# A streaming encoder layer: band writes and bias loads queued behind a weight load, a value tile released earlier, one attention step placed behind the next rows

## The chip, the cores and the metric

One NeuronCore of a Trainium2 chip runs the whole program. The metric is the device time of one execution in microseconds (us), lower is better. Of several executions the median counts.

## The reference

One layer of an encoder with three head groups reads the same normalised rows (2048 prompt rows and 8 x 16 sample rows of width 1024):

```python
qa, ka, va, ga, qb, kb, vb, gb, qm, gm = _project(x, g_pre, w_in)      # RMSNorm, then one matmul
oa = _band_attention(qa, ka, va, A_LEFT_CHUNKS, _relpos_bias(rel_bias_a, d), None)   # 6 heads, 64 + 512 keys
ob = _band_attention(qb, kb, vb, B_LEFT_CHUNKS, _alibi_bias(d), sink_b)              # 6 q heads, 2 kv heads
om = _attn_core(qm, mk, mv, None, None, None)                          # mk, mv from 256 memory rows
y  = x + rmsnorm(concat([oa * silu(ga), ob * silu(gb), om * silu(gm)]) @ w_out, g_post)
```

The sample rows do the same against caches of keys and values (512 cached keys for A, 128 for B, 256 memory keys for M). Outputs are y, and the new keys and values.

## The kernel before, in words

The prompt rows go in four groups of 512; group 0 carries the 128 sample rows too. Every float32 product is made as three products of rounded halves, so each weight tile of 128 x 1024 comes as a *pair*: `load_w` (L145 to L156) issues the DMA into `wraw` on SyncE's queue (SPq, L152), ScalarE copies the rounded upper half into `whl` (L153), and VectorE or GpSimd in turn subtracts to get the lower half (L154). There are three `wraw` and three `whl` buffers.

A group has a *dense* lane (V: value projections, Pa and Pb: key, query and gate of a head pair, K: the B keys, N: the next group's row scales, L: `load_rows` of the next group, Q: its memory queries, O: output projection) and an *attention* lane (M: memory, Sa and Sb: sample attention of a pair of A or B heads, Aa and Ab: prompt attention). The tables `DENSE` and `ATTENTION` (L43 to L50) list the steps, `AFTER` (L56 to L59) says which must be done before a step, and two generators are interleaved by their estimated cost. A scheduler in the build then fixes the order on each engine: it takes what is emitted first and is ready first in its own model of time. On the chip each engine runs its instructions strictly in that order.

Ahead of group 0 stand `first_rows`, the memory's keys and values (`memory_keys`, L328 to L343) and the sample's memory attention (`sample_m`). `memory_keys` makes two value tiles of 128 x 256 in PSUM: `split_v` (L255) makes their halves `mV` by ScalarE (L237) and VectorE (L238), and `store_T` (L296) copies them for the output (`stgT`, L298). Projections share two PSUM buffers of one tag (`psN`, `psT`), so a third tile starts only when the first is read out.

The A bias depends on the distance alone. `bands()` (L369 to L371) writes six bands `skew_d` of 128 x 768 in DRAM from a row `e_d`, and skewed reads of it give the bias tiles: `nbs` in `sample_a` (L719 to L727, 17 small loads) and `nbA` in `attn_a` (L756 to L760, four loads of 64 x 576), with three `nb` buffers. `load_rows` (L462) of group 1 loads eight column blocks (`xk`, two buffers), scales and splits them into `xn`, in place of the old rows. `next_scales` loads the next group's rows (`xt`), squares them on ScalarE and ends with small TensorE products `rb` (L183).

Names in the order rows below: `sa`, `sb` are scores, `ss` the sample's scores, `pt` and `spt` transposes, `oa`, `ob`, `so` values, `kta` and `vta` the sample's cached keys and values.

Of the kernel before, what the change touches and what calls it, by code (L numbers as in the profile page):

```python
# [53 lines left out]
PIECE = 6  # L54

AFTER = {"X1": "Aa0", "X2": "Aa1", "K0": "Aa0", "V1": "Aa0", "Pa2": "Aa1", "C0": "K0 V1 Ab0 Ab1 Ab2",  # L56
         "E0": "M0 M1 Aa0 Aa1 Ab0 Ab1 Ab2", "Aa0": "F0 V0 X0 Pa0", "Aa1": "V0 X1 Pa1", "Aa2": "V1 X2 Pa2", "Sa0": "V0 Pa0", "Sa1": "V0 Pa1", "Sa2": "V1 Pa2"}
for _j in range(3):
    AFTER[f"Ab{_j}"] = AFTER[f"Sb{_j}"] = f"K0 V1 Pb{_j}"  # L59
W_AT = {name: i for i, name in enumerate(W_TILES)}  # L60
# [3 lines left out]
def encoder_step(ctx, tc, x_p, x_s, xT0, xT, mem, memT, wt, wm, g_pre, g_mem, g_post, rel_rev, sink,  # L64
# [3 lines left out]
    pe, act, dve, pool, sp = nc.tensor, nc.scalar, nc.vector, nc.gpsimd, nc.sync  # L68
# [73 lines left out]
    vctx_d = [drp.tile([128, 4, 256], F32, name=f"vctx{i}") for i in range(6)]  # L142


    def load_w(src, hl=None):  # L145

        raw = wrawp.tile([128, 1024], F32, tag="wraw", name="wraw")
        if hl is None:
            hl = whlp.tile([128, 2, 1024], F32R, tag="whl", name="whl")
        eng = (dve, pool)[turn["s"] % 2 if turn["s"] > 4 else 0]  # L150
        for m in [slice(0, 1024)] if turn["s"] else [slice(0, 512), slice(512, 1024)]:
            sp.dma_start(out=raw[:, m], in_=src[:, m])  # L152
            act.activation(hl[:, 0, m], raw[:, m], AF.Copy)  # L153
            eng.tensor_tensor(hl[:, 1, m], raw[:, m], hl[:, 0, m].bitcast(F32), ALU.subtract)  # L154
        turn["s"] += 1
        return hl  # L156
# [139 lines left out]
    def store_T(dst, ps, n, scale=1.0):  # L296
        t = sbp.tile([128, 640], F32, tag="sb", name="stgT")
        act.activation(t[:, :n], ps, AF.Copy, scale=scale)  # L298
        sp.dma_start(out=dst, in_=t[:, :n])

    def memory_load():
        t = [xp.tile([128, D], F32, tag="x", name="mT") for _ in range(2)]
# [25 lines left out]
    def memory_keys(st):  # L328

        rk = sbp.tile([128, 640], F32, tag="sb", name="rk")[:, :256]  # L330
        act.activation(rk, row_factors(st, 2)[:, :256], AF.Copy)
        for p in range(2):
            w = load_w(wm[p])
            ps = run(project_T(w, memhl, 0, 256))
            t = sbp.tile([128, 640], F32, tag="sb", name="mkn")[:, :256]
            dve.tensor_tensor(t, ps[:, :256], rk, ALU.mult)
            split_k(mK[:, p], slice(0, 256), t)
            sp.dma_start(out=mkT[p], in_=t)
        ws = [load_w(wm[2]), load_w(wm[3])]
        for i in range(2):  # L340
            ps = run(project_N(ws, lambda a, k: memhl[:, a, k, i * 128:(i + 1) * 128]))
            split_v([mV[:, 0], mV[:, 1]], i, ps, st[:, i:i + 1])
            store_T(mv[i * 128:(i + 1) * 128], ps[:, :256], 256, st[:, i:i + 1])  # L343

    def toeplitz(h, n, c0, c1):

# [199 lines left out]
    def xg(g):  # L546
        return xnT[min(g, 1)]
# [67 lines left out]
    memory_keys(mst)  # L615
    for p in range(2):
        sample_m(p, *qg[p][1:])
    bands()

    bctx = None  # L620
    for g in range(NG):
# [14 lines left out]
        def block_v(slots, half):  # L636
            ws = [weights("v", half, r) for r in range(2)]
            for i in range(5 if g == 0 else 4):
                ps = yield from project_N(ws, lambda a, k: xg(g)[:, a, k, i * 128:(i + 1) * 128])
                if i == 4:  # L640
                    vsm = gr[:, 1280:1536] if half else mo[:, 4, 4:6].rearrange("p a b -> p (a b)")
                    act.activation(vsm, ps[:, :256], AF.Copy, scale=rs_rows[:, 4:5])
                    if half == 0:
                        sp.dma_start(out=avs[:, 0:256], in_=vsm)
                    else:
                        sp.dma_start(out=avs[:, 256:384], in_=vsm[:, 0:128])
                        sp.dma_start(out=bvs, in_=vsm[:, 128:256])
                    return [vsm[:, 0:128], vsm[:, 128:256]]
                split_v(slots, i, ps, rs_rows[:, i:i + 1] if g == 0 else None)
                if g == NG - 1:  # L650
                    t = xp.tile([128, 640], F32, tag="xk", name="stgN", bufs=2)
                    act.activation(t[:, :256], ps[:, :256], AF.Copy)
                    r0 = i * 128
                    if half == 0:
                        sp.dma_start(out=av[r0:r0 + 128, 0:256], in_=t[:, 0:256])
                    else:
                        sp.dma_start(out=av[r0:r0 + 128, 256:384], in_=t[:, 0:128])
                        if i == 3:
                            sp.dma_start(out=bv, in_=t[:, 128:256])
            return []  # L660
# [57 lines left out]

        def sample_a(pr, Q, G, ksm, vsm):  # L719
            bias = nbp.tile([128, 640], F32, tag="nb", name="nbs")  # L720
            sp.dma_start(out=bias[:, 512:576], in_=mask_new)
            for h in range(2):
                for b in range(4):
                    r = 32 * b + 16 * h
                    sp.dma_start(out=bias[r:r + 16, 0:512], in_=toeplitz(2 * pr + h, 16, 0, 512))
                    sp.dma_start(out=bias[r:r + 16, 512 + 16 * b:528 + 16 * b],
                                 in_=toeplitz(2 * pr + h, 16, 512, 528))  # L727
            kt, vt = {}, {}

            def kts(hf, b):  # L730
                if b % 2 == 0:
                    if pr == 0 or (pr == 1 and b == 2):
                        kt[0] = spare_load(b // 2, ckaT[pr, 2 * hf + b // 2])
                        kt[0] = kt[0].rearrange("p (b c) k -> p b c k", b=2)
                    else:
                        t = wrawp.tile([128, 1024], F32, tag="wraw", name="kta")
                        sp.dma_start(out=t, in_=ckaT[pr, 2 * hf + b // 2])
                        kt[0] = t.rearrange("p (b k) -> p b k", b=2)
                return kt[0][:, b % 2]

            def vts(hf, b, t):
                if b % 2 == 0 and t == 0:
                    v = xp.tile([128, D], F32, tag="x", name="vta")
                    sp.dma_start(out=v, in_=cva[pr, 2 * hf + b // 2])
                    vt[b // 2] = v.rearrange("p (b t d) -> p b t d", b=2, t=4)
                return vt[b // 2][:, b % 2, t]

            return sample_attn(pr, Q, G, kts, vts, 512, (ksm, vsm), bias, None)

        def attn_a(pr, q, G, slot, vcur, vctx=None):  # L750
            nb, held = [], {}

            def weigh(i0, h):
                if not nb:
                    for hh in range(2):
                        t = nbp.tile([128, 640], F32, tag="nb", name="nbA")  # L756
                        for p, c in ((0, 0), (64, 64)):
                            pool.memset(t[p:p + 64, 576 * (p == 0):][:, :64], BIG)
                            sp.dma_start(out=t[p:p + 64, c:c + 576], in_=toeplitz(2 * pr + hh, 128, c, c + 576)[p:p + 64])
                        nb.append(t)  # L760
                st = stp.tile([128, 16], F32, tag="st", name="sta")
                for i in (i0, i0 + 1):
# [454 lines left out]
```

## Time and profile before

| | |
|---|---|
| median of 3 runs | 1175.23 us (1174.24 to 1175.70) |
| the profiled execution's own time | 1173.39 us |
| its span | 1171.4 us |
| TensorE matmul (PE) busy | 1121.5 us, 96% |
| VectorE (DVE), ScalarE (ACT), GpSimd (POOL) busy | 803.8, 729.3, 313.2 us |
| mean granted TensorE clock | 0.991 of full speed |

The profile is one execution; 2.0 us of its own time lie outside the span. An engine's "idle before" is the wait ahead of an instruction, with the instruction that ended it. PEclk is the granted share of TensorE's full clock. SPq rows are DMA issues on SyncE's queue, and a DMA row of the chain of waits lasts from issue to landing.

### The profile page before, as it was taken

Reading aid. Unit: us, or ns where it says so; the run is one execution under the profiler, and the core shown is the slowest. Engines: PE = TensorE matmul, PEld = TensorE weight load, DVE = VectorE, ACT = ScalarE, POOL = GpSimd, SP = SyncE. Lnnn points to the kernel's source line nnn. Section 1 sums busy time; section 2 is a strip of 40 time slices with the busy share of each in tenths; the row PEclk is TensorE's granted clock in tenths of the full one; section 3 lists DMA queues with packets and bytes.
Section 4 is the critical chain, followed back from the end, with each engine's and each line's share of the span. In section 5 each row is a group of like instructions: output and inputs, shape, how many; then the busy total and the mean of one; then the engine's idle time right before and its main releaser. Section 6 shows DMA issues by size and latency. Waiting matters only on the chain.

```text
span 1171.4 us, 21035 instructions
## 1 busy us (share of the span) xinstructions
PE 1121.5 (96%) x7794; PEld 1015.7 (87%) x7794; DVE 803.8 (69%) x1859; ACT 729.3 (62%) x1688; POOL 313.2 (27%) x259
## 2 busy tenths in 40 slices
PE   7999999899799999999999999999999999999997
PEld 6989889798589988998789988988879988898797
DVE  7738666777675347678988337679987337678854
ACT  7647556666474556566886455557886456567762
POOL 4211111121321551221421451221421541212320
PEclk9999999899999999999999999999999999999999
DMA  7672555324721584233331394333321483232222
GB/s 281 213 262 102 161 180 185 120 74 160 238 88 55 170 323 155 91 117 110 111 93 37 105 373 152 92 125 102 112 91 37 125 298 93 80 114 83 67 82 95
DMA packets 62622, 162.64 MB, mean 139 GB/s; under 512 B 8492, under 2 KB 19762, under 8 KB 62520
## 3 DMA queue, kind: packets, MB, share of 16 engines
q1 hardware_dynamic: 58776, 151.87, 38.5%
q0 software_dynamic: 3744, 9.44, 2.7%
q8 instruction: 61, 1.00, 0.3%
q14 instruction: 41, 0.34, 0.1%
HBM read 140.16 MB, written 23.48 MB: 140 GB/s over the span
## 4 chain that ended last, share of the span: by engine, by line
PE 72%; DVE 8%; ACT 7%; issue 6%; DMA 4%; POOL 2%; SPq 1%; DVEq 0%; POOLq 0%; ACTq 0%
PE psT L213 31%; PE psN L226 20%; PE pt L273 5%; PE oa L286 4%; PE sa L267 4%; DMA xt<-in_x_p 2%; PE ob L286 2%; ACT whl L153 1%; DVE whl L154 1%; DMA wraw<-in_wt 1%; DVE sh L235 1%; PE ss L384 1%; POOL whl L154 1%; ACT sh L234 1%; DMA skew_d<-e_d 1%
## 5 line engine op out<-in xcount | busy, mean ns | idle before, releaser
L213 PE MATMUL psT<-xn,whl 128*128 128x512 f32 (+2 forms) x2400 | 521.5, 367 | 12.3 <-ACT whl L153 5.6
L213 PEld LDWEIGHTS psT<-xn,whl 128*128 128x128 f32 x2400 | 407.2, 190 | 74.3 <-ACT whl L153 5.6
L154 POOL TENSOR_TENSOR whl<-wraw,whl 128x1024 fp32r<-128x1024 f32 x63 | 153.1, 2431 | 338.3 <-ACT whl L153 309.6
L226 PE MATMUL psN<-whl,sh 128*128 128x256 f32 x1296 | 160.5, 281 | 3.3 <-DVE sh L927 2.2
L226 PEld LDWEIGHTS psN<-whl,sh 128*128 128x128 f32 x1296 | 154.3, 188 | 5.7 <-DVE sh L927 3.4
L153 ACT ACTIVATE whl<-wraw 128x1024 fp32r<-128x1024 f32 (+1 forms) x132 | 138.3, 1048 | 27.5 <-PE psN L226 14.5
L226 PE MATMUL psN<-whl,xn 128*128 128x256 f32 x1080 | 145.9, 285 | 5.9 <-ACT stgT L298 3.8
L226 PEld LDWEIGHTS psN<-whl,xn 128*128 128x128 f32 x1080 | 135.7, 191 | 9.0 <-ACT stgT L298 4.0
L235 DVE TENSOR_TENSOR sh<-pt,sh 128x512 fp32r<-128x512 f32 (+2 forms) x206 | 122.2, 625 | 14.3 <-ACT sh L234 13.4
L234 ACT ACTIVATE sh<-pt 128x512 fp32r<-128x512 f32 (+2 forms) x206 | 103.7, 548 | 36.5 <-PE pt L273 27.0
L154 DVE TENSOR_TENSOR whl<-wraw,whl 128x1024 fp32r<-128x1024 f32 (+1 forms) x69 | 96.3, 1396 | 21.6 <-ACT whl L153 21.0
L775 ACT ACTIVATE sba<-sba,sta 128x640 f32<-128x640 f32 (+2 forms) x96 | 73.1, 762 | 56.1 <-DVE sta L773 55.9
L773 DVE CUSTOM_DVE_ANT_0 sba<-sa,nbA 128x640 f32<-128x640 f32 (+2 forms) x96 | 70.7, 737 | 32.6 <-PE sa L267 31.7
L665 POOL TENSOR_TENSOR mo<-sums,gr 128x256 f32<-128x256 f32 (+1 forms) x38 | 36.9, 972 | 194.3 <-DVE sums L294 176.2
L286 PE MATMUL oa<-sh 128*128 128x256 f32 (+1 forms) x504 | 75.2, 281 | 1.3 <-DVE sh L235 0.9
L286 PEld LDWEIGHTS oa<-sh 128*128 128x128 f32 x504 | 68.5, 192 | 4.6 <-DVE sh L235 1.9
L273 PE MATMUL pt<-ident,sba 128*128 128x128 f32 x420 | 63.9, 276 | 4.0 <-DVE sh L235 2.6
L526 DVE TENSOR_TENSOR mo<-psN,gpost 128x256 f32<-128x256 f32 x52 | 22.0, 423 | 61.3 <-ACT junk L525 61.1
L267 PE MATMUL sa<-sh,qr 128*128 128x320 f32 (+2 forms) x240 | 51.6, 325 | 4.6 <-DVE sta L773 2.4
L273 PEld LDWEIGHTS pt<-ident,sba 128*128 128x128 f32 x420 | 48.5, 141 | 7.6 <-DVE sh L235 2.8
L859 ACT ACTIVATE sbb<-sbb,stb 128x256 f32<-128x256 f32 (+1 forms) x96 | 47.2, 493 | 11.8 <-DVE stb L857 11.7
L525 ACT ACTIVATE junk<-psN 128x256 bf16<-128x256 f32 x52 | 20.0, 384 | 50.4 <-PE psN L226 50.3
(285 smaller groups left out, 1615.2 us busy)
## 6 DMA issues: line engine op xcount, KB each, us to landing
wraw<-in_wt SPq DMA_DIRECT2D x128, 512.0 KB, 3.8
xr<-in_x_p SPq DMA_DIRECT2D x16, 512.0 KB, 5.0
nbA<-skew_d SPq DMA_DIRECT2D x48, 144.0 KB, 2.8
vta<-in_cva SPq DMA_DIRECT2D x12, 512.0 KB, 5.4
xt<-in_x_p SPq DMA_DIRECT2D x12, 512.0 KB, 4.7
out_y_p<-mo SPq DMA_DIRECT2D x12, 512.0 KB, 4.4
vctx<-sh SPq DMA_DIRECT2D x9, 512.0 KB, 5.0
kctx<-sh SPq DMA_DIRECT2D x9, 512.0 KB, 4.0
```

The lines of the kernel that those rows point to most:

```text
L153: act.activation(hl[:, 0, m], raw[:, m], AF.Copy)
L154: eng.tensor_tensor(hl[:, 1, m], raw[:, m], hl[:, 0, m].bitcast(F32), ALU.subtract)
L213: pe.matmul(ps[:, :n], w[:, a, k * 128:(k + 1) * 128], src[:, b, k, c0:c0 + n], start=(i == 0), stop=(i == 23))
L226: pe.matmul(ps[:, :256], stat(a, k), w[:, b, (k % 4) * 256:(k % 4 + 1) * 256], start=(k == ks[0] and i == 0), stop=(k == ks[-1] and i == 2))
L234: act.activation(hi, src, AF.Copy)
L235: eng.tensor_tensor(lo, src, hi.bitcast(F32), ALU.subtract)
L267: pe.matmul(out[:, c:c + n], q[:, part, qc:qc + 128], kt[:, h, kc:kc + n], start=part == h, stop=part != h)
L273: pe.transpose(pt[:, i * 128:(i + 1) * 128], b, ident)
L286: pe.matmul(o[:, oc:oc + w], v, pt[:, part, c:c + w], start=(first and i == 0), stop=(i == n - 1), skip_group_check=True)
L773: dve.tensor_tensor_reduce(sb[:, :nk], s[:, c0:c0 + nk], nb[h][:, 640 - nk:], 1.0, 3.0e38, ALU.add, ALU.min, st[:, e:e + 1])
L775: act.activation(sb[:, :nk], sb[:, :nk], AF.Exp, bias=st[:, e:e + 1], scale=-1.0, accum_out=st[:, 2 + e:3 + e])
L859: act.activation(dst, dst, AF.Exp, bias=st[:, i:i + 1], scale=-1.0, accum_out=st[:, 4 + i:5 + i])
```

## The change

`load_w` remembers its last DMA. `bands()` moves from ahead of group 0 into the first value projection, behind its two weight loads; its writes, the `nbs` loads and the `nbA` loads are then queued on SyncE no earlier than the last weight load traced before them (`tc.issue_after`, issue order only). In `memory_keys` the value tile is first copied out, scaled, and the halves are split from that copy. The sample attention of the last A pair (`Sa2`) is emitted only after `L0`, the load of group 1's rows.

```diff
-... "Sa2": "V1 Pa2"}
+... "Sa2": "V1 Pa2 L0"}
...
-            sp.dma_start(out=raw[:, m], in_=src[:, m])
+            last["w"] = sp.dma_start(out=raw[:, m], in_=src[:, m]).ins
...
         sp.dma_start(out=dst, in_=t[:, :n])
+        return t
...
-            split_v([mV[:, 0], mV[:, 1]], i, ps, st[:, i:i + 1])
-            store_T(mv[i * 128:(i + 1) * 128], ps[:, :256], 256, st[:, i:i + 1])
+            t = store_T(mv[i * 128:(i + 1) * 128], ps[:, :256], 256, st[:, i:i + 1])
+            split_v([mV[:, 0], mV[:, 1]], i, t)
...
-    bands()
...
             ws = [weights("v", half, r) for r in range(2)]
             for i in range(5 if g == 0 else 4):
+                if g == 0 and half == 0 and i == 0:
+                    with tc.issue_after(last["w"]):
+                        bands()
...
         def sample_a(pr, Q, G, ksm, vsm):
             bias = nbp.tile([128, 640], F32, tag="nb", name="nbs")
+            with tc.issue_after(last["w"]):
 ...
...
                             pool.memset(t[p:p + 64, 576 * (p == 0):][:, :64], BIG)
+                            with tc.issue_after(last["w"]):
 ...
```

What the scheduler makes of it differs on every engine. Three places matter. The first is SyncE's queue around the bands. `in_wm` are the memory's weight tiles, the first two `in_wt` behind them those of the first value projection. Before, from the write of `e_d`:

```order
L367 DMA e_d<-gr 6x768
L721 DMA nbs<-in_mask_new 128x64
L152 DMA wraw<-in_wm 128x1024
L371 DMA skew_d<-e_d 128x768
L152 DMA wraw<-in_wm 128x1024
L371 DMA skew_d<-e_d 128x768 x5
L725 DMA nbs<-skew_d 16x512
```

Now:

```order
L370 DMA e_d<-gr 6x768
L154 DMA wraw<-in_wm 128x1024 x2
L154 DMA wraw<-in_wt 128x1024 x2
L374 DMA skew_d<-e_d 128x768 x3
L341 DMA out_mkT<-mkn 128x256
L374 DMA skew_d<-e_d 128x768 x2
L341 DMA out_mkT<-mkn 128x256
L439 DMA mo<-in_ckmT 128x4x256
L374 DMA skew_d<-e_d 128x768
L154 DMA wraw<-in_wt 128x1024 x2
L301 DMA out_mv<-stgT 128x256 x2
L154 DMA wraw<-in_wt 128x1024
```

Before, twelve `nbs` loads stood between the last band and the first value weight, and four more with three `nbA` loads ahead of the second. Now both value weights stand ahead of the bands, the next two weights (`K0`'s and the query's behind it) stand behind all six, and the `nbs` loads come after a fifth.

The second is ScalarE's order around the memory's values. `whl` is a weight copy, `mV` half of a value tile's split, `stgT` its copy for the output. Before:

```order
L153 ACTIVATE whl<-wraw 128x1024
L252 ACTIVATE mK<-mkn 64x256 x2
L237 ACTIVATE mV<-psN,nstm 128x2x64 x2
L153 ACTIVATE whl<-wraw 128x1024
L298 ACTIVATE stgT<-psN,nstm 128x256
L237 ACTIVATE mV<-psN,nstm 128x2x64
L153 ACTIVATE whl<-wraw 128x1024
L237 ACTIVATE mV<-psN,nstm 128x2x64
L298 ACTIVATE stgT<-psN,nstm 128x256
```

Now:

```order
L155 ACTIVATE whl<-wraw 128x1024
L254 ACTIVATE mK<-mkn 64x256 x2
L300 ACTIVATE stgT<-psN,nstm 128x256
L236 ACTIVATE mV<-stgT 128x2x64 x2
L155 ACTIVATE whl<-wraw 128x1024
L300 ACTIVATE stgT<-psN,nstm 128x256
L400 ACTIVATE ssb,sst<-ss,sst 128x256
L236 ACTIVATE mV<-stgT 128x2x64 x2
L416 ACTIVATE spT<-spt 128x256
L155 ACTIVATE whl<-wraw 128x1024
L400 ACTIVATE ssb,sst<-ss,sst 128x256
```

The last reader of the first value tile's PSUM was a `stgT` behind the second value weight's copy; it is now a `stgT` ahead of it. The third weight copy shown is `K0`'s.

The third is TensorE where group 1's first projection (`psT` 128x512) begins, among the last steps of `Ab2` (`ob`), `Sa2` (`ss`, `spt`) and `Aa2` (`sa`). Before:

```order
L267 MATMUL sa<-sh,qr 128x256 x2
L286 MATMUL ob<-sh 128x256
L286 MATMUL ob<-sh 128x128 x2
L408 MATMUL spt<-ident,ssb 64x128
L412 MATMUL spt<-ident,ssb 128x128 x4
L384 MATMUL ss<-kta,qd_122 32x512 x4
L387 MATMUL ss<-ksm,qd_122 128x64
L286 MATMUL ob<-sh 128x256 x6
L286 MATMUL ob<-sh 128x128 x2
L213 MATMUL psT<-xn,whl 128x512 x7
L267 MATMUL sa<-sh,qr 128x128 x2
L213 MATMUL psT<-xn,whl 128x512 x3
```

Now:

```order
L269 MATMUL sa<-sh,qr 128x256 x2
L288 MATMUL ob<-sh 128x256
L288 MATMUL ob<-sh 128x128 x2
L411 MATMUL spt<-ident,ssb 64x128
L415 MATMUL spt<-ident,ssb 128x128 x4
L215 MATMUL psT<-xn,whl 128x512 x2
L387 MATMUL ss<-kta,qd_122 32x512 x4
L390 MATMUL ss<-ksm,qd_122 128x64
L215 MATMUL psT<-xn,whl 128x512 x5
L288 MATMUL ob<-sh 128x256 x6
L288 MATMUL ob<-sh 128x128 x2
L269 MATMUL sa<-sh,qr 128x128 x2
```

The new rows' first products move ahead of the sample's second score group and of the last `ob` products; the rest of `Sa2` stands where it stood. Ahead of this piece, one ALiBi score group (`sb`, eight products) and two sample value groups, which stood among the last projections of group 0, now stand behind them.

## Rows read from the trace of the kernel before

**Rows 1.** The page: the span, and TensorE's busy time and instructions.

```profile
span 1171.4 us, 21035 instructions
PE 1121.5 (96%) x7794; PEld 1015.7 (87%) x7794; DVE 803.8 (69%) x1859; ACT 729.3 (62%) x1688; POOL 313.2 (27%) x259
```

**Rows 2.** Windows: stretch, busy us (instructions) by engine, PEclk, DMA share, GB/s.

```profile
60.00:64.00 4.00, 3.02 (x15) 3.02 (x16) 1.62 (x2) 2.50 (x5) 2.37 (x1) 0.65 0.96 353
200.00:216.00 16.00, 11.59 (x79) 9.68 (x78) 13.21 (x42) 11.31 (x34) 4.70 (x4) 0.79 0.43 141
286.00:328.00 42.00, 33.41 (x228) 23.85 (x227) 30.96 (x72) 23.06 (x49) 14.43 (x16) 0.96 0.65 217
340.00:600.00 260.00, 255.90 (x1689) 231.61 (x1688) 177.94 (x392) 164.72 (x365) 78.72 (x59) 1.00 0.41 136
600.00:870.00 270.00, 264.19 (x1733) 238.51 (x1732) 192.13 (x422) 174.40 (x386) 80.94 (x67) 1.00 0.39 130
870.00:1130.00 260.00, 251.98 (x1702) 229.39 (x1702) 175.52 (x403) 166.38 (x387) 73.61 (x54) 0.99 0.34 112
```

**Rows 3.** Timeline of TensorE, 47 to 69 us: start, us, what [idle before].

```profile
47.96 2.76 PE L213 MATMUL psT<-sh,whl 128*128 128x256 f32 x22
...
51.21 5.92 PE L226 MATMUL psN<-whl,sh 128*128 128x256 f32 x48
60.98 7.11 PE L226 MATMUL psN<-whl,xn 128*128 128x256 f32 x45 [3.84 <-ACT stgT L298]
67.92 0.38 PE L412 MATMUL spt<-ident,ssb 128*128 128x128 f32 x2
68.23 0.64 PE L384 MATMUL ss<-mo,qd 128*32 128x256 f32 x8
```

**Rows 4.** Timeline of ScalarE, 53 to 61 us.

```profile
53.91 1.06 ACT L153 ACTIVATE whl<-wraw 128x1024 fp32r<-128x1024 f32 x1 [3.67 <-DMA wraw<-in_wt]
...
59.51 1.06 ACT L153 ACTIVATE whl<-wraw 128x1024 fp32r<-128x1024 f32 x1 [1.59 <-DMA wraw<-in_wt]
60.47 0.46 ACT L298 ACTIVATE stgT<-psN,nstm 128x256 f32<-128x256 f32 x1
```

**Rows 5.** The chain of waits, 36 to 62 us: start, us, what.

```profile
38.88 8.88 DMA skew_d<-e_d
...
54.16 5.24 DMA wraw<-in_wt
```

**Rows 6.** Tile `skew_d`, 0 to 70 us: its issues, then timeline of SyncE's queue at 50 us.

```profile
L371 SPq DMA_DIRECT2D skew_d<-e_d x6: 504/598/1417, 34.3 to 38.9; - x6
...
50.03 0.37 SPq L152 DMA_DIRECT2D wraw<-in_wt  x1
```

**Rows 7.** Timelines of GpSimd and VectorE, 42 to 48 us: lower halves of two weights.

```profile
42.18 2.41 POOL L154 TENSOR_TENSOR whl<-wraw,whl 128x1024 fp32r<-128x1024 f32 x1 [4.37 <-ACT whl L153]
...
46.89 1.22 DVE L154 TENSOR_TENSOR whl<-wraw,whl 128x1024 fp32r<-128x1024 f32 x1
```

**Rows 8.** The page, DMA issues: KB each, median us from issue to landing.

```profile
wraw<-in_wt SPq DMA_DIRECT2D x128, 512.0 KB, 3.8
```

**Rows 9.** Timeline of TensorE, 115 to 308 us.

```profile
115.88 0.42 PE L267 MATMUL sa<-sh,qr 128*128 128x128 f32 x2
...
273.08 1.10 PE L267 MATMUL sb__3274<-sh,qr 128*128 128x128 f32 x8
...
294.59 1.06 PE L384 MATMUL ss<-kta,qd 128*32 128x512 f32 x8 [1.34 <-DVE sta L773]
...
296.81 1.84 PE L213 MATMUL psT<-xn,whl 128*128 128x512 f32 x7
...
307.08 0.48 PE L426 MATMUL spt<-ident,ssb 128*128 128x128 f32 x1 [3.01 <-DVE ssb L423]
```

**Rows 10.** Timeline of TensorE at 185 us, and tile `xt`, 180 to 215 us.

```profile
184.82 1.08 PE L420 MATMUL so<-vta,spT 128*32 128x128 f32 x32
...
L172 ACT ACTIVATE xt<-xt x4: 1058/1062/1064, 191.9 to 207.4; 128x1024 f32<-128x1024 f32 x4
```

More of the change, by code (lines that the diff above doesn't have):

```diff
@@ L56 @@
 AFTER = {"X1": "Aa0", "X2": "Aa1", "K0": "Aa0", "V1": "Aa0", "Pa2": "Aa1", "C0": "K0 V1 Ab0 Ab1 Ab2",
-         "E0": "M0 M1 Aa0 Aa1 Ab0 Ab1 Ab2", "Aa0": "F0 V0 X0 Pa0", "Aa1": "V0 X1 Pa1", "Aa2": "V1 X2 Pa2", "Sa0": "V0 Pa0", "Sa1": "V0 Pa1", "Sa2": "V1 Pa2"}
+         "E0": "M0 M1 Aa0 Aa1 Ab0 Ab1 Ab2", "Aa0": "F0 V0 X0 Pa0", "Aa1": "V0 X1 Pa1", "Aa2": "V1 X2 Pa2", "Sa0": "V0 Pa0", "Sa1": "V0 Pa1", "Sa2": "V1 Pa2 L0"}
 for _j in range(3):
@@ L142, in encoder_step @@
     vctx_d = [drp.tile([128, 4, 256], F32, name=f"vctx{i}") for i in range(6)]
+    last = {}
     def load_w(src, hl=None):
@@ L720, in sample_a @@
             bias = nbp.tile([128, 640], F32, tag="nb", name="nbs")
[L721 to L727, printed above, removed]
+            with tc.issue_after(last["w"]):
+                sp.dma_start(out=bias[:, 512:576], in_=mask_new)
+                for h in range(2):
+                    for b in range(4):
+                        r = 32 * b + 16 * h
+                        sp.dma_start(out=bias[r:r + 16, 0:512], in_=toeplitz(2 * pr + h, 16, 0, 512))
+                        sp.dma_start(out=bias[r:r + 16, 512 + 16 * b:528 + 16 * b],
+                                     in_=toeplitz(2 * pr + h, 16, 512, 528))
             kt, vt = {}, {}
@@ L758, in weigh @@
                             pool.memset(t[p:p + 64, 576 * (p == 0):][:, :64], BIG)
-                            sp.dma_start(out=t[p:p + 64, c:c + 576], in_=toeplitz(2 * pr + hh, 128, c, c + 576)[p:p + 64])
+                            with tc.issue_after(last["w"]):
+                                sp.dma_start(out=t[p:p + 64, c:c + 576],
+                                             in_=toeplitz(2 * pr + hh, 128, c, c + 576)[p:p + 64])
                         nb.append(t)
```

## The prediction

> **What bounds the kernel now.** I read the page first. TensorE is busy for 1121.5 of 1171.4 us [rows 1], so all its idle time together is 49.9 us, and no change of order can win more than that and what the clock loses after an idle stretch. The question is where those 50 us lie. The windows answer it [rows 2]. From 340 to 1130 us TensorE idles 4.10, 5.81 and 8.02 us in three stretches of some 260 us: many waits, none long. Three places ahead of that are worse. At 57 us it waits 3.84 us. Between 200 and 216 us it idles 4.41 us at a mean granted clock of 0.79. Between 286 and 328 us it idles 8.59 us at 0.96. The change works on the first and the third.
>
> The first wait is read from the timeline and the chain together. The memory's value projections run from 51.21 for 5.92 us and end at 57.13. The next projection, the first value tile of group 0, starts at 60.98, released by `stgT` [rows 3]. It needs a PSUM buffer that `stgT` reads last. ScalarE runs in order, and `stgT` (60.47) stood behind the copy of the second value weight (59.51), which had waited for its DMA; the first value weight's copy had waited 3.67 us the same way [rows 4]. Why the weights were late is in the chain: SyncE's queue stood at the bias loads until the last band landed, 8.88 us after its issue; the first value weight was issued only at 50.03, and the second at 54.16, to land after 5.24 us [rows 5, 6]. So the cause is a queue, two engines away from the one that idles. The wait costs more than itself. After it the granted clock is 0.65 for 4 us [rows 2], between the two levels of 1.2 and 2.4 GHz, and 45 products take 7.11 us where 48 equal ones took 5.92 just before [rows 3]: 45 x 0.1233 = 5.55, so 1.56 us more. The place is worth 3.84 + 1.56 = **5.4 us**.
>
> **The change part by part.**
>
> *Bands and bias loads behind the weights, and the value tile released early.* These two remove the same wait and are costed together. The first value weight can be issued when its raw buffer is free, which is when the weight three before it has its lower half: 42.18 + 2.41 = 44.6 [rows 7]. Its copy must also wait for the `whl` buffer of the second key weight, which TensorE reads until 47.96 + 2.76 = 50.7 [rows 3]. At 1.06 us for the copy and 1.22 for the lower half it is ready at 53.0, ahead of 57.13. The second value weight is issued at 46.89 + 1.22 = 48.1, lands some 3.8 us later [rows 8], and its copy waits for the `whl` buffer that the value products release after 36 of 48, at 55.7. Copied at 56.8, with its lower half on GpSimd at 59.2 (2.41). TensorE reaches its first use of that half after 14 products, at 58.9. New wait: 0.3 us. The first `stgT` now needs only the first value tile (54.2) and holds nothing up. So TensorE goes on at 57.13. Removed: 5.4; added: 0.3.
>
> What is late next is the weight behind the bands, `K0`'s. Six bands at about 0.6 us of queue each [rows 6] and three other issues of about 0.5 follow the second value weight, so it is issued at about 53.6. It lands at 57.4 by the median load [rows 8], at 62.5 if it takes as long as the last band, 8.88 [rows 5]. Its copy stands on ScalarE ahead of the split of group 0's first value tile, and TensorE needs that tile's PSUM after 48 products, a transpose pair and four scores: 57.13 + 5.92 + 0.38 + 0.64 = 64.1 [rows 3]. Copy (1.06), an exponential and two half splits (each taken as the 0.46 of `stgT`) take 2.5 us, so the load must be there at 61.6. The wait is thus between nothing and 0.9 us; I take 0.5. Sum of the place: -5.4 + 0.3 + 0.5 = **-4.6 us**.
>
> The Trainium skill (DMA: Bandwidth & Descriptors, section "Queues, rings and completion order") says that on each DMA engine descriptors are consumed in ring order. This speaks against putting a weight behind 2.4 MB of bands: by it `K0`'s load lands no earlier than they do, the wait is 0.9, and the sum of the place -4.2. The trace agrees as far as it goes: the weight issued behind three `nbA` loads took 5.24 us where the median is 3.8 [rows 5, 8]; no row has a weight behind six bands.
>
> The split of the value tile from its copy changes no count that matters: the same two half copies per tile on ScalarE and two subtractions on VectorE. The `nbs` and `nbA` loads of group 0 now issue some 15 us later, about 60 to 73 us; the first prompt scores of A stood at 115.88 [rows 9], and 5 us earlier there are still some 40 us of projections to cover them. If that cover went, each bias would cost its landing of a few us. In later groups four `nbA` loads pass the row loads of `finish`; they are needed some 30 us after. I cost all this at nothing. The memory keys for the second pair of the sample (`ckmT`) stand behind five bands, issued at 52.6, needed at about 64.7; that load has 12 us, and I cost it at nothing too.
>
> *`Sa2` behind `L0`.* The order shows that this moves little. Seven of the new rows' products pass the second score group (1.06 us) and the last `ob` products; in exchange one ALiBi score group (1.10) and two sample value groups with their transposes now cover the time between the last old-row product and the first new one, which stood at 296.81 [rows 9]. That is about 1 us more cover in front of a wait that is bound by loading and splitting rows; the four moved `nbA` loads also leave a crowded stretch. I take **-1.0 us**. The bounds are wide, since no row shows this order: the whole stretch is worth 8.59 + 0.04 x 42 = 10.3 us [rows 2], which could vanish, or as much could be added.
>
> *The rest of the order.* Everything behind is scheduled anew. Between 200 and 216 us TensorE waits for work that follows, on ScalarE, the squares of the next rows (four of 1.06 us, 191.9 to 208.5, each behind a load [rows 10]). These loads start once the sample's values are read, at 184.82 + 1.08 = 185.9, and four in a chain take 22.6 us however TensorE is ordered. I take 0, with -7.8 (4.41 and 0.21 x 16 of clock) as the lower bound and some 3 us more as the upper. For 340 to 1130 us I take 0 as well, give or take 4 of the 17.9 us of waits.
>
> Sum: -4.6 - 1.0 = -5.6 us against this execution's own time of 1173.39 (span 1171.4 and 2.0 around it) gives 1167.8. The median of the runs lies 1.84 above this execution, so the forecast is **1169.6 us**.
>
> **The rivals.**
>
> *More is won than the first place.* In the new order projections stand between the B scores and the sample's scores where 200 to 216 us had attention alone. If a third of the 7.8 + 10.3 us of these two stretches goes, the time is 1169.6 - 6.0 = 1163.6. For it: waits such as 1.34 and 3.01 us [rows 9] are in-order ones, with other work queued behind. Against it: both stretches hang on chains of loads.
>
> *The wait comes back at the next weight.* If `K0`'s load lands 4 us after 61.6, TensorE waits 4 us at the third value tile, its clock falls as it did at 60 us, and the place gives -5.4 + 0.3 + 4.0 + 1.56 = 0.5: with the -1.0 of `Sa2`, 1174.7. For it: the DMA share there is already 0.96 [rows 2], and the bands are added. Against it: that needs 12 us from issue to landing where the last band took 8.88.
>
> *Slower: the new rows starve TensorE.* Place: group 1's first projection. It now stands ahead of the sample's second score group, so if the second row block lands late (its load is queued behind an `nbA` load that waits for the bias buffer of `Ab2`), TensorE stands there in order with that cover behind it. If the waits of 286 to 328 us double, this is +10.3 in place of -1.0: 1175.2 - 4.6 + 10.3 = 1180.9. It turns the result to slower from 7 us of added wait on (4.6 + 2.35). Against it: only one block's load is behind that buffer, and the rest stands as before.
>
> *Nothing moves but the queue.* The order rows rule out that the bands stay where they were, but `Sa2` may well gain nothing: 1170.6, inside the forecast's range.
>
> **How the numbers follow.** Forecast 0.57, more won 0.20, wait comes back 0.14, slower 0.09. The forecast's own range is 1166 to 1173.5. With the other cases, 1163.0 to 1176.0; the slower rival and the better half of the first stay outside. A difference of 0.2%, 2.35 us, is about what this measurement can tell. Faster by more: 0.53 of the forecast's 0.57 and all of the first rival, 0.73. Within it: the rest of the forecast and most of the second, 0.17. Slower: 0.10.
>
> **What would show it.** The wait of 3.84 us ahead of the first value tile is gone and the granted clock at 60 us is near 1; the value weights are issued at about 45 and 48 us, the bands from there to 54. The first transposes of the sample's memory attention come at about 61 us. Wrong would be: a weight copy on ScalarE waiting over 2 us for its DMA between 57 and 66 us with TensorE idle behind it; an idle sum of over 10 us between the last old-row product and group 1's second projection; or an undisturbed start with the gain given back by 230 us.

## The result and the profile after

The changed kernel takes 1163.01 us in the median (1160.82 to 1165.53) against 1175.47 for the kernel before (1174.24 to 1177.7) on the same chip: a ratio of 0.9893 (95% interval 0.9866 to 0.9919), 12.5 us less. The forecast was 1169.6 us, 5.9 us less than this: its sign was right, its size less than half of what came. The profiled execution of the change takes 1162.07 us of its own, 11.3 less than the one of before.

The page of the changed kernel, against [rows 1]:

```profile
span 1160.0 us, 20998 instructions
...
PE 1118.3 (96%) x7794; PEld 1014.5 (87%) x7794; DVE 794.7 (69%) x1859; ACT 730.8 (63%) x1688; POOL 313.9 (27%) x259
```

TensorE idles 41.7 us in place of 49.9. The windows, in the places of [rows 2] moved by what had been won till there (stretch, its length, busy time of each engine, granted clock, DMA share, GB/s):

```profile
60.00:64.00 4.00, 4.00 (x40) 3.29 (x42) 0.42 (x1) 0.38 (x1) 0.20 (x2) 1.00 1.02 334
64.00:72.00 8.00, 5.85 (x48) 4.72 (x48) 3.61 (x11) 3.50 (x10) 0.00 (x0) 0.79 0.85 277
194.00:210.00 16.00, 14.37 (x106) 13.99 (x106) 12.07 (x34) 10.53 (x27) 4.68 (x4) 1.00 0.43 142
279.00:321.50 42.50, 35.51 (x221) 24.98 (x222) 32.71 (x81) 24.45 (x56) 13.55 (x18) 0.88 0.61 204
```

At 60 us the idle time is gone, but the 8 us behind it have 2.15 us of it and a clock of 0.79. The stretch at 200 us idles 1.63 us at full clock where it idled 4.41 at 0.79. The stretch at 286 us, which the table was to help, idles 7.0 of 42.5 us at 0.88, where it was 8.59 of 42 at 0.96: nothing is won there.

The first place is read from TensorE's timeline (start, length, what; in brackets the wait ahead and what ended it):

```profile
51.52 5.92 PE L228 MATMUL psN<-whl,sh 128*128 128x256 f32 x48
57.28 3.46 PE L228 MATMUL psN<-whl,xn 128*128 128x256 f32 x28
...
66.22 0.64 PE L387 MATMUL ss<-mo,qd 128*32 128x256 f32 x8 [1.37 <-ACT ssb L400]
67.61 0.33 PE L429 MATMUL spt<-ident,ssb 128*128 128x128 f32 x1 [0.74 <-DVE ssb L426]
```

The 3.84 us of [rows 3] are gone: the first value tile follows directly. Two new waits stand nine microseconds later. ScalarE's and SyncE's timelines name the cause:

```profile
64.66 1.06 ACT L155 ACTIVATE whl<-wraw 128x1024 fp32r<-128x1024 f32 x1 [3.28 <-DMA wraw<-in_wt]
65.62 0.46 ACT L400 ACTIVATE ssb<-ss,sst 128x256 f32<-128x256 f32 x1
```

```profile
44.95 3.84 SPq L154 DMA_DIRECT2D wraw<-in_wt  x2
48.84 1.84 SPq L374 DMA_DIRECT2D skew_d<-e_d  x3
...
54.65 0.48 SPq L374 DMA_DIRECT2D skew_d<-e_d  x1
56.04 1.32 SPq L154 DMA_DIRECT2D wraw<-in_wt  x2
```

The value weights go out at 45 and 48 us as forecast, the bands from 48.84 to 55.1, and K0's weight at 56.04. It lands only at 64.6: the chain of waits of the changed kernel has

```profile
56.04 8.54 DMA wraw<-in_wt
```

Its copy holds ScalarE, and the exponential behind that copy (65.62) is what TensorE waits for at 66.22. A weight copy that waits over 2 us for its DMA between 57 and 66 us was one of the prediction's signs of being wrong; this one waits 3.28.

Where the whole difference lies is best seen by products. TensorE makes the same 7521 products in both kernels (the page's 7794 count two records for each of 273 small ones), and at some places of its queue the same *set* of them has been done. At 342 and 465 that holds to within ten products and one, which moves those two columns by 0.1 to 0.2 us in the kernels with the early release. The table gives what a kernel gained (-) or lost (+) against the trace of before between such places, from the start times of the n-th product; the times of before are in the second row. Two executions of the changed kernel are shown, the second taken with the experiments; the other rows are experiments below.

| products | to 300 | to 342 | to 465 | to 1895 | to 2398 | to 4162 | to 5842 | to 7500 | sum |
|---|---|---|---|---|---|---|---|---|---|
| before, us | 55.33 | 65.92 | 80.82 | 286.57 | 372.17 | 645.72 | 908.35 | 1161.80 | |
| changed | +0.30 | -5.64 | +3.77 | -5.47 | +0.07 | -2.29 | -3.37 | +1.53 | -11.1 |
| changed, again | +1.49 | -5.64 | +2.01 | -2.16 | +0.59 | -2.70 | -3.49 | +2.02 | -7.9 |
| hold on all bias loads | -0.13 | -4.08 | 0.00 | +0.91 | -1.11 | -3.90 | -3.40 | +2.20 | -9.5 |
| hold, sample's alone | +1.67 | -4.09 | 0.00 | +0.83 | +0.63 | +0.35 | +0.51 | +1.53 | +1.4 |
| hold, prompt's alone | +1.49 | -4.10 | -0.14 | +1.03 | -1.29 | -1.35 | -3.37 | +2.92 | -4.8 |
| hold, prompt's, g = 0 | -0.07 | -2.70 | 0.00 | +0.32 | +0.26 | -0.13 | +0.67 | -0.20 | -1.9 |
| hold, prompt's, g = 2 | +0.68 | -1.34 | 0.00 | +0.83 | +0.79 | +1.06 | -3.39 | +1.23 | -0.1 |
| hold but for last group | -0.15 | -4.09 | -0.08 | +0.64 | +0.10 | -4.06 | -3.39 | +0.29 | -10.7 |
| bands and release, no hold | +1.43 | -5.64 | +5.98 with the next | | +7.49 | -0.72 | +0.37 | +0.05 | +9.0 |

A column has to be read with its noise. Up to 300 products all kernels do the same work, and still stand up to 1.8 us apart, for the most part because in some executions the granted clock falls once between 14 and 45 us (0.94 over that stretch in place of 1.00). The last column holds such a difference too: between 1090 and 1120 us the clock is 0.89 for the sample's hold, the prompt's and g = 2, and 0.94 for the kernel before. And the trace of before is one of its faster executions: 1173.39 us of its own, where the 55 executions timed beside the change and the experiments ran from 1172.87 to 1180.77. So the sums show up to some 6 us less than the timed runs, and the columns, not the sums, carry what follows.

Three columns were not forecast: groups 1 and 2 (products 2398 to 5842) win 2.3 to 2.7 and 3.4 to 3.5 us in the changed kernel, group 3 gives 1.5 to 2 back. TensorE's order in groups 1 and 2 is the same, product for product, in the changed kernel and with the hold on all loads, on the prompt's alone or on all but the last group. What group 1 wins by it still goes from 1.4 to 4.1 us: three of those five traces have a wait for a load (`sh<-kctx`) of 0.9 to 1.7 us in it, and the two that win most have none.

### The profile page after: what moved, and what is told of

Same layout as the page of the kernel before. It is cut to its first block, busy times and chain, and to the rows that moved or that the text cites. A ratio compares the mean times of both kernels' runs of the same rounds, so it can differ in the third digit from the quotient of the medians.

```text
span 1160.0 us, 20998 instructions
## 1 busy us (share of the span) xinstructions
PE 1118.3 (96%) x7794; PEld 1014.5 (87%) x7794; DVE 794.7 (69%) x1859; ACT 730.8 (63%) x1688; POOL 313.9 (27%) x259
## 4 chain that ended last, share of the span: by engine, by line
PE 83%; DVE 6%; ACT 4%; DMA 4%; issue 2%; SPq 0%; POOL 0%; DVEq 0%; POOLq 0%; ACTq 0%
PE psT L215 37%; PE psN L228 23%; PE pt L275 6%; PE oa L288 4%; PE sa L269 4%; PE ob L288 2%; PE om L288 1%; PE sm L269 1%; DMA xk<-in_xT 1%; PE ss L387 1%; DVE sh L237 1%; ACT whl L155 1%; PE so L423 1%; DVE whl L156 1%; DMA wraw<-in_wt 1%
## 5 line engine op out<-in xcount | busy, mean ns | idle before, releaser
L215 PE MATMUL psT<-xn,whl 128*128 128x512 f32 (+2 forms) x2400 | 527.0, 368 | 12.6 <-ACT whl L155 5.9
L275 PE MATMUL pt<-ident,sba 128*128 128x128 f32 x420 | 67.3, 275 | 0.4 <-DVE sh L237 0.4
```

What stands on the lines that cost most here:

```text
L215: pe.matmul(ps[:, :n], w[:, a, k * 128:(k + 1) * 128], src[:, b, k, c0:c0 + n], start=(i == 0), stop=(i == 23))
L275: pe.transpose(pt[:, i * 128:(i + 1) * 128], b, ident)
```

## The experiments

In their rows the line numbers differ by a few from those of the change. The first four set this theory against its rivals: each part pays where its own order differs, and the later groups win by the bias loads' hold. Each set of four ran on a chip of its own with the kernel before beside it, so sets are compared by their ratios to it.

**The hold alone.**

```diff
+            with tc.issue_after(last["w"]):
                 (the nbs loads, and the nbA loads, as in the change)
```

> The kernel before with one part of the change alone: the bias loads of the sample (nbs) and of the prompt (nbA, all groups) are held behind the last weight load issued; the bands, the memory values and the table stay as they were. TensorE's order is then the one of before up to the last old-row products at about 300 us, and the one of the change in groups 1 and 2. Theory 1 (the gain of the later groups comes from their own new order, which the bias loads bring): the first 280 us as before (wait of 3.84 us at 57 us and 4.4 us idle at 200 to 216 us still there), groups 1 to 3 as in the changed kernel, -4.6 us in all (-3 to -6). Rival (the later gain is carried on from the lead of group 0): 0, within 1.5 us of before.

Measured: 1164.58 us, ratio 0.9888 (0.9873 to 0.9903). This is as much as the whole change gives, and 12.8 us by the medians where 4.6 were expected. Groups 1 and 2 won 3.90 and 3.40 us as said. What was expected wrongly is the first place: the 3.84 us went too, with the bands still ahead of the value weights. That is 4.1 of the 8 us between; 2.8 are the distance of the traced executions from the medians.

**Bands, release and table without the hold.** In the change, the two `issue_after` blocks around the bias loads are taken out, the one around `bands()` stays.

> The change without the hold on the bias loads: bands behind the value weights, the value tile released early, the table as changed. TensorE's order is the changed one up to about 72 us, an order of its own to about 360 us, and that of before behind it. Theory 1: the first place as in the changed kernel (-5.3 us at the first transposes of the sample's memory attention, some -1.8 us left at 81 us), something between -1 and -7 at 365 us by what its own order does at 200 us, and nothing further: -2 to -6 in all, no gain behind 365 us (within 1 us). Rival (a lead from group 0 is what pays later): -9 to -11, growing by 4 to 5 us behind 365 us.

Measured: 1182.26 us, ratio 1.0039 (1.0026 to 1.0053): slower than before. The rival falls (nothing is won behind 2398 products), and so does the size that the theory gave. It wins 5.64 us at the first place, loses 6.0 up to product 1895 and 7.5 more up to 2398. The largest wait behind the kernel's first instructions, in TensorE's timeline:

```profile
335.74 1.78 PE L268 MATMUL sm<-mK,xn 128*128 128x256 f32 x8 [3.68 <-ACT xn L247]
```

These scores wait for the first queries of the new rows, whose projection ran late: TensorE starves at the new rows, as the prediction's slower rival had it, though not in the changed kernel.

**The change without the table's entry.**

```diff
-"Sa2": "V1 Pa2 L0"
+"Sa2": "V1 Pa2"
```

> The change with the old table (Sa2 without L0). TensorE's order is that of the change but for 92 places between about 250 and 330 us. Theory 1: the table is worth little either way, and this kernel stands within 1.5 us of the changed one (-10 to -12.5 against before); the idle time between 270 and 327 us tells which way. Rival (the new order of the table is where the gain comes from): 3 us or more slower than the changed one. If it is faster by over 1 us, the table costs time.

Measured: 1165.46 us, 0.9894 (0.9879 to 0.9909), against 0.9893 and 0.9887 for the changed kernel in its two sets. The entry is worth nothing that can be told. Put alone into the kernel before, it moves no product in TensorE's order; that kernel was not timed.

**K0's weight ahead of the bands.**

```diff
                 if g == 0 and half == 0 and i == 0:
+                    last["k0"] = weights("k", 0)
                     with tc.issue_after(last["w"]):
                         bands()
...
-            w = weights("k", p)
+            w = last.pop("k0", None) or weights("k", p)
```

> The changed kernel with the load of K0's weight issued ahead of the six bands too (they stand behind it on SyncE). Everything behind about 135 us keeps the changed kernel's order. Theory 1 (the 3.6 us given back between 60 and 80 us are K0's weight behind the bands: 2.1 us of waits and 1.7 us of clock): the copy of that weight on ScalarE no longer waits for its DMA, the waits of 1.37 and 0.74 us at 66 and 67.6 us go, the clock stays up, and the kernel is 3 to 4 us faster than the changed one, some -15 us against before. Rival (the wait is ScalarE's order or the sample's own memory attention): under 1 us faster. If the gain is lost by 200 us, the stretch there hangs on loads after all.

Measured: 1166.07 us, 0.99 (0.9883 to 0.9917): nothing won. The mechanism was right, the copy no longer waits:

```profile
59.35 1.05 ACT L155 ACTIVATE whl<-wraw 128x1024 fp32r<-128x1024 f32 x1
```

But the next load behind the bands takes the place, the memory keys of the sample's second pair:

```profile
73.69 0.64 PE L387 MATMUL ss<-mo,qd 128*32 128x256 f32 x8 [1.30 <-DMA mo<-in_ckmT]
```

Two more waits, of 0.83 and 0.43 us, come at 96 and 98 us. The profiles of the changed kernel have no such waits there. Against the first of them this kernel gains 2.6 us between products 300 and 520, against the second, whose clock did not fall at 68 us, 0.9; against either it gives 1.8 back by 638. The bands are 6 x 384 KB in a place where the DMA share is 1.02 (the window at 60 us above); what is put in front of them changes who is late.

**The two holds apart.** The next four ask which loads do it.

```diff
 (sample's alone: nbs)                 (prompt's alone: nbA)
+with tc.issue_after(last["w"]):       +with tc.issue_after(last["w"]):
```

> The kernel before with the hold on the sample's bias loads (nbs) alone. TensorE's order is that of before in every place, so only SyncE's queue is changed: the two value weights stand ahead of the bias loads that wait for the bands. Theory 2 (the first place is a matter of this queue alone; bands and the early release add nothing to it): the wait of 3.84 us at 57 us goes and the clock does not fall behind it, -4 to -5 us at 62 us, kept to the end, nothing further: -4.3 in all (-3 to -6). Rival (the gain needs the bands behind the weights too): the first value weight lands late behind the bands, under 2 us won.

Measured: 1173.82 us, 0.9972 (0.9958 to 0.9985), 3.3 us won. Every product is in the order of before, so this is the queue alone, 4.09 us in the column "to 342" and nothing behind. The value weights go out at

```profile
46.05 3.85 SPq L153 DMA_DIRECT2D wraw<-in_wt  x2
```

> The kernel before with the hold on the prompt's bias loads (nbA) alone. TensorE's order is that of before up to about 300 us and that of the first experiment (bias loads alone) behind. Theory 2: the first place stays as before (wait of 3.84 us, clock fall), groups 1 and 2 win 7.6 us through their new order, group 3 gives 1.5 to 2 back: -5.3 in all (-4 to -7.5). Rival (the later groups win because they start 4 us earlier, or with other loads in flight): under 2 us won.

Measured: 1166.45 us, 0.9894 (0.9876 to 0.9912): nearly the whole gain, more than either theory said. The first wait goes here too, although twelve sample loads still stand ahead of the first value weight:

```profile
48.89 0.37 SPq L153 DMA_DIRECT2D wraw<-in_wt  x1
...
51.22 0.37 SPq L153 DMA_DIRECT2D wraw<-in_wt  x1
```

Three `nbA` loads no longer stand ahead of the second weight; it goes out at 51.2 in place of 54.16 [rows 5], and that is early enough. So either hold removes the wait, and their gains must not be added.

**The hold but for the last group.**

```diff
-with tc.issue_after(last["w"]):
+with (tc.issue_after(last["w"]) if g in (1, 2) else contextlib.nullcontext()):
     (nbA; nbs held as in the change; nothing else changed from before)
```

> The kernel before with the hold on the sample's bias loads, and on the prompt's in groups 1 and 2 only. TensorE's order is that of the first experiment up to the last 440 products. Theory 2: as the first experiment, but the 1.5 to 2 us that it gives back between 897 and 1005 us (first bias loads of group 3 late: a wait of 1.6 us) stay won: 1 to 2 us below that experiment, some -13.5 to -14.5 against before. Rival (the time given back lies in the order, not in the late bias): no difference from the first experiment within 0.7 us.

Measured: 1162.57 us (1161.41 to 1163.46), 0.9864 (0.9846 to 0.9882). It is the fastest ratio of all, without bands moved, early release or table, and 2.8 us under the changed kernel timed beside it (1164.45 to 1165.91, no overlap). The wait that it avoids is seen in the changed kernel's timelines of SyncE and TensorE:

```profile
925.01 2.39 SPq L766 DMA_DIRECT2D nbA<-skew_d  x4
```

```profile
935.38 5.86 PE L215 MATMUL psT<-xn,whl 128*128 128x512 f32 x24 [1.59 <-ACT stgN L657]
```

Four bias loads stand there among the outputs and weights that are due; in this kernel they have gone by 859 us and the projection starts with no wait.

```profile
857.76 1.08 SPq L763 DMA_DIRECT2D nbA<-skew_d  x2
```

```profile
935.99 7.26 PE L215 MATMUL psT<-xn,whl 128*128 128x512 f32 x30
```

The chain of waits of the changed kernel has no DMA between 922 and 940 us, so the wait is not a load that came late. What differs is ScalarE's order. Changed kernel, then this one:

```profile
934.00 1.05 ACT L155 ACTIVATE whl<-wraw 128x1024 fp32r<-128x1024 f32 x1
934.95 0.38 ACT L657 ACTIVATE stgN<-psN 128x256 f32<-128x256 f32 x1
```

```profile
935.57 0.36 ACT L654 ACTIVATE stgN<-psN 128x256 f32<-128x256 f32 x1
...
936.19 1.05 ACT L155 ACTIVATE whl<-wraw 128x1024 fp32r<-128x1024 f32 x1
```

The projection waits for that `stgN`, and with the hold a weight copy of 1.05 us stands ahead of it.

**The changed kernel again**, in the set of the last three.

> The changed kernel itself on the chip of the other experiments, so that they can be set against it. By theory 2 its bands, early release and table add nothing to the bias loads: within 1.5 us of the first experiment's ratio (0.9888), in all -11.5 to -14. Rival (the whole change is worth more than its bias loads): 2 us or more below it.

Measured: 1165.35 us, 0.9887 (0.9869 to 0.9905), the same as the hold alone. Its trace differs from the first one of the same program at 200 us. The first trace has

```profile
201.73 0.38 PE L288 MATMUL oa<-sh 128*128 128x256 f32 x1 [1.34 <-ACT sh L236]
202.40 0.46 PE L185 MATMUL rb<-dg,ones 128*128 128x128 f32 x2 [0.29 <-DVE dg L184]
202.62 3.21 PE L215 MATMUL psT<-xn,whl 128*128 128x384 f32 x17
```

and the second

```profile
202.93 0.38 PE L288 MATMUL oa<-sh 128*128 128x256 f32 x1 [2.30 <-ACT sh L236]
```

The windows from 198 to 218 us, of the first and then of the second:

```profile
198.00:218.00 20.00, 18.37 (x139) 17.33 (x138) 14.60 (x44) 14.19 (x38) 4.16 (x3) 1.00 0.30 100
```

```profile
198.00:218.00 20.00, 17.41 (x117) 16.70 (x116) 13.63 (x41) 12.69 (x33) 4.13 (x3) 0.91 0.24 83
```

The wait of 1.34 us left the clock up, that of 2.30 was followed by a fall worth 0.09 x 20 = 1.8 us. So of the 5.47 us in the column "to 1895" 3.3 belong to that execution, the fall and the longer wait (0.96) among them. The first trace is the exception: in all four other traces with this order at 200 us (this one, without the table, K0's weight first, and the change but for the last group) the clock falls there.

**One group alone, and the first alone.**

```diff
-with tc.issue_after(last["w"]):
+with (tc.issue_after(last["w"]) if g == 2 else contextlib.nullcontext()):   (then: g == 0)
```

> The kernel before with the hold on the prompt's bias loads in the third group (g = 2) alone. TensorE's order is that of before but for its places 4591 to 5842 of 7523, some 709 to 908 us. Theory 3 (a group wins by the order that the scheduler finds for it, wherever the rest stands): nothing before 709 us (the wait of 3.84 us at 57 us stays), 4.9 us won between 709 and 882 us, 1.1 given back by 908, and that kept: -3.8 in all (-2.5 to -4.5). Rival (the gain needs the earlier start, or the loads of all groups moved): under 1.5 us won.

Measured: 1171.01 us, 0.9962 (0.9947 to 0.9976), 4.5 us. TensorE's products are in another order between 4591 and 5842 alone, and but for 1.3 us at the first place, where this kernel is the one before (last section), the time is won there alone: 4.85 us from product 4590 to 5620, 1.09 back to 5842, as said. The groups of waits of TensorE between these products, in the kernel before and then here:

```profile
PE pt L273 <- DVE sh L235: 1.3, 1, 1.3
PE sb__9140 L267 <- DVE stb L857: 0.9, 1, 0.9
PE psN L226 <- DVE sh L927: 0.8, 1, 0.8
PE psT L213 <- DVE qr L245: 0.7, 1, 0.7
PE psT L213 <- DVE xn L245: 0.6, 1, 0.6
PE ob L286 <- ACT sh L234: 0.3, 1, 0.3
```

```profile
PE oa L288 <- DVE sh L237: 0.8, 1, 0.8
PE psN L228 <- DVE sh L931: 0.4, 1, 0.4
PE oa L288 <- DVE sums L296: 0.2, 1, 0.2
```

Six waits of 4.6 us became three of 1.4. None ends at a DMA: what goes is waiting for VectorE's and ScalarE's halves and scores. In the kernel before neither TensorE nor VectorE, ScalarE or GpSimd waits for a DMA between 708 and 884 us, so it is not an earlier or later landing that was saved there, and what is left is the engines' order: which instruction stands where. What moved first on SyncE are the loads of this group's first bias tiles; before they stood among the last weights of the group ahead, now behind them (first before, then this experiment):

```profile
596.00 1.09 SPq L759 DMA_DIRECT2D nbA<-skew_d  x2
...
606.46 1.09 SPq L759 DMA_DIRECT2D nbA<-skew_d  x2
```

```profile
678.35 2.52 SPq L762 DMA_DIRECT2D nbA<-skew_d  x4
...
701.43 1.11 SPq L762 DMA_DIRECT2D nbA<-skew_d  x2
```

> The kernel before with the hold on the prompt's bias loads in the first group alone. TensorE's order is that of before in every place. Theory 3: three bias loads leave the place between the two value weights on SyncE, which is enough: the wait of 3.84 us goes although the sample's sixteen loads stand where they stood, -4.2 us at 62 us and nothing further, -3 to -4.5 in all. Rival (the whole 11 us of the prompt's hold come from moving the first group): -8 or more.

Measured: 1173.57 us, 0.9987 (0.9973 to 1.0), 1.5 us, less than said. The order is that of before, and only the first place gains: 2.70 us by the trace, as a wait of 1.53 us is left there. The trace of g = 2, which has the order and the queue of before in that place, waits 2.63 us in place of 3.84 and stands at -1.34; against it the hold gains 1.4 us, as timed. The rival is out.

**Two combinations.** The change with the hold left out for `nbA` in the last group; and the hold but for the last group with the early release added.

> The changed kernel with the hold on the prompt's bias loads left out in the last group only. TensorE's order is that of the change but for 230 places of the last group. Theory 3: the wait of 1.6 us at 935 us goes and is not paid elsewhere, 1.5 to 2.8 us below the changed kernel (ratio to before 0.9862 to 0.9876). Rival (the gain of the seventh experiment was the run of its executions): within 0.7 us of the changed kernel.

Measured: 1161.79 us (1157.11 to 1163.55), 0.9878 (0.9858 to 0.9898). The last column falls from +2.02 to +0.16, so the wait is gone, but the ratio is not distinguishable from that of the changed kernel; inconclusive.

> The seventh experiment (hold on the bias loads but for the last group, bands where they were) with the early release of the memory's value tile added. TensorE's order differs between places 342 and 2350 alone. Theory 3: the bands stay early, so K0's weight is not behind them and no 2.15 us of waits with 1.7 of clock come at 66 us; the waits of 0.2 and 0.4 us at 59 to 61 us go; what the other order of the first group does at 200 us is open. 0 to 2 us below the seventh experiment (ratio to before 0.985 to 0.9865). Rival (the early release brings an order that starves TensorE in the first group, as with bands and release alone): 2 us or more above it.

Measured: 1166.84 us, 0.9928 (0.9908 to 0.9948) against 0.9864 without the release, 7.5 us lost: the rival. It wins 5.64 us at the first place (without it 4.09) and loses 6.4 between products 1895 and 2398, with the same two waits as bands and release alone (3.7 us for the queries of the new rows, 2.3 for their rows). The early release pays 1.5 us where it works, and brings an order that costs more elsewhere unless the bands' move and the hold are both beside it: with either alone (here, and in the second experiment) time was lost.

## Why the prediction was wrong in size

**The first place: right in its cause, wrong in what was needed.** "Removed: 5.4" came out at 5.34 (product 342 starts at 60.58 in place of 65.92); the 0.3 us for the lower half did not come. But the bands' move was costed together with the bias loads, and the experiments part them: the bias loads alone give 4.1 of it, even one of the two holds does.

**K0's weight: mis-sized.** It stood at 0.5 us, with an end of 0.9. It measured 2.1 us of waits and 8 x 0.21 = 1.7 of clock in the first trace, 2.0 and no fall in the second: the columns "to 465". Two numbers failed. The issue came at 56.0, not 53.6, and the load took 8.54 us, near the 8.88 of the last band [rows 5], which I had kept as the far end. The rival "the wait comes back" named the mechanism; of its price (4.0 us of wait and 1.56 of clock) 3.8 us came in the first trace and 2.0 in the second. The Trainium skill (DMA: Bandwidth & Descriptors, section "Queues, rings and completion order") has descriptors consumed in ring order on each DMA engine; the trace agrees, as the weight issued behind six bands took 8.54 us and the one issued ahead of them was ready for its copy at 59.35. The rule's side of the argument should have been taken, with the price of the last band and not with 0.9 us.

**The table: -1.0, measured 0.** Ratios of 0.9887 to 0.9893 with it and 0.9894 without.

**200 to 216 us: 0, measured -3.1 in the first trace and -0.6 in the second** (products 1297 to 1895). The order with `rb` and the new products behind the waiting attention does help, as the rival "more is won" said: between these products kernels in the order of before stand at +0.3 to +1.0. How much hangs on whether the clock falls.

**A place that was not costed: -1.7.** In the column "to 1895" the changed kernel stands at -5.5 and -2.2. Of this 1.7 us are won between products 1116 and 1158 (168 to 176 us), in every one of the five traces with the change's order, and no wait of TensorE goes there. The rows are the scores of the sample's second pair, four products of 32 columns with two records each. In the kernel before the first and the last of them stand apart, with value products between; in the changed kernel all four run side by side (before, then the change):

```profile
171.74 1.05 PE L384 MATMUL ss<-kta,qd 128*32 128x512 f32 x2
...
175.13 0.59 PE L384 MATMUL ss<-mo,qd 128*32 128x512 f32 x1
```

```profile
166.85 0.62 PE L387 MATMUL ss<-kta,qd 128*32 128x512 f32 x2
...
167.32 0.60 PE L387 MATMUL ss<-mo,qd 128*32 128x512 f32 x2
```

They take from 171.74 to 175.72 us there and from 166.85 to 167.92 here. A change of order can thus win time in which the profile shows TensorE busy.

**The step that failed: "For 340 to 1130 us I take 0 as well, give or take 4 of the 17.9 us of waits."** It is -3.9 and -3.4 us in groups 1 and 2, and 2.2 back in group 3, with the hold alone; in the changed kernel -2.3, -3.4 and +1.5. The zero was an absence of an argument. The order was known to be new in those groups, all their waits ended on engines and so could be moved by it, and the loads that I costed at nothing because they were "needed some 30 us after" bring another order when they are held. I priced the transfers and not the order. What they cost in the last group, a wait of 1.6 us, I had not seen either, and it is an order too, ScalarE's. The margin of 4 reached as far as the changed kernel's sum there, -4.1, but the forecast was built on the 0.

By the columns of the second trace, the first place up to product 465 holds 3.6 us, the rest of group 0 1.6 and the groups behind 4.2; in the first trace it is 1.9, 5.4 and 4.1. That is 9.4 of the 12.2 us (without the first column) by which the median of this set fell, and 11.4 of 12.5 in the other. The 1 to 3 us that remain are not placed: they are within the distance between the traced execution of before and its medians. No second trace of it was taken, but three experiments have its order behind the first place, and from product 342 on their traces stand 0.9 us (g = 0), 3.9 (the sample's hold) and, up to product 4162, 2.7 (g = 2) behind it: it is a fast one there. Also open is why the scheduler finds the better order when these loads come later; shown is that the order goes with the hold, that group 2 gains 3.4 to 4.1 us in every kernel that has it and stands within 0.7 of nothing in the three that don't, and that it needs nothing else.

## What to carry to other kernels

A hint to a scheduler can change the order far behind it, and has to be costed there: compare the orders of all engines, and where they differ in a stretch whose waits end on engines, put a range on it, not zero. Here some 4 us were won in the changed kernel, and 7 with the hold but for the last group, where 17.9 us of waits stood. Of a change in several parts try each alone, for here the hold was worth the whole, the table's entry nothing, and the early release lost time in two of its three combinations. What is put behind a large transfer must be followed to the next two loads, not one.

## What was not expected of the hardware

One program's executions can differ by a clock fall: in the changed kernel a wait of 1.34 us at 202 us left the granted clock at 1.00 and one of 2.30 in the same place was followed by 0.91 over 20 us. At 66 us waits of 1.37 and 0.74 us were followed by 0.79 over 8 us in one trace, waits of 1.22 and 0.75 by 1.00 in the other. The same code ahead of 57 us gave a wait of 3.84 us in the trace of before [rows 3] and 2.63 in that of the hold for g = 2, where the second value weight's copy began 0.54 us earlier and TensorE came 0.68 us later:

```profile
60.44 1.92 PE L228 MATMUL psN<-whl,xn 128*128 128x256 f32 x14 [2.63 <-ACT stgT L300]
```

Differences under 3 us between two single traces need the product-by-product columns, or the timed runs, before a cause is put to them.
